# Mixer of a hybrid encoder: three engines in a written order, the softmax's sum and maximum in one instruction, the gates' first products inside attention

## The chip, the cores and the metric

The kernel runs on one core of one Trainium2 chip. The metric is the device time of one execution in microseconds. A core has five engines with a queue each: TensorE (PE, matmuls; its weight loads are shown as PEld), VectorE (DVE), ScalarE (ACT), GpSimd (POOL) and SyncE (SP, which here only issues DMAs). An engine works through its queue in order and waits at an instruction until what it needs has arrived. SBUF is the memory on the chip, and PSUM is where matmuls write, here as 8 banks.

## The reference

Two layers, each of three residual steps, and a final RMSNorm; 512 tokens of 1024 numbers, all in float32:

```python
def mixer(h, w_in, gate_bias, rpb, w_na_out, w_f_out, w_o):
    z = h @ w_in                      # q, k, v: 512 columns each, uf: 512, ga and gf: 1024 each
    ...
    y_na = neighbourhood_attention(q, k, v, rpb) @ w_na_out
    y_f = fourier_mix(uf) @ w_f_out   # real part of a 2-D DFT, 4 groups of 128 channels
    g_na = jax.nn.sigmoid(ga + gate_bias[0])
    g_f = jax.nn.sigmoid(gf + gate_bias[1])
    return (g_na * y_na + g_f * y_f) @ w_o

for l in range(DEPTH):                # DEPTH = 2
    x = x + 0.5 * swiglu(rms_norm(x, ffn1_norm[l]), ffn1_w_in[l], ffn1_w_out[l])
    x = x + mixer(rms_norm(x, mix_norm[l]), ...)
    x = x + 0.5 * swiglu(rms_norm(x, ffn2_norm[l]), ffn2_w_in[l], ffn2_w_out[l])
return rms_norm(x, final_norm)
```

SwiGLU has a hidden width of 2816. The attention has 8 heads of 64; a token of the 8 x 64 grid looks at 8 rows and 16 columns around it, and a learned bias by relative position is added to the scores before the softmax.

## The kernel before, in words

**Precision.** Each float32 operand is split into a high part, which ACT rounds to the matmul's input format, and a low part, which DVE takes as the difference (`split`, lines 297 to 300: L299 is the ACT half, L300 the DVE half). A product is three matmuls, high by high, high by low and low by high (`mm3`, L293 to L295). So every weight granule (128 x 1024, 512 KB) is loaded, rounded by ACT and subtracted by DVE before TensorE can use it, and so is every activation.

**The stream of weights.** `Stream` holds all granules in the order of their use. `next()` hands out one and prepares (`Item.prep`: the split, and a sum of two granules where one is needed, L173) two more ahead (AHEAD); `fetch` issues the loads of FETCH = 8 granules beyond what is prepared. Loads are DMAs on SP's queue (L150); sums of two granules are done either by DVE or by an accumulating DMA on POOL's queue (L152 and L182), which first waits for the plain load. Split granules lie in three rotating pairs (`wp`), or, for the four V granules (`kept=True`), in general slots, of which there are 23 of 4 KB per partition (`kp`). Most large products go by Strassen's scheme: seven products of half-size blocks instead of eight, with an order of their own (`ORDER`, products 1, 5, 2, 6, 7, 3, 4), where sums of the input blocks are products' operands and the outputs are added to and subtracted from each other.

**A layer.** FFN 1, mixer, FFN 2. FFN's output product ends with Strassen's product 4 in three chunks (`m == 4`), after which the last quarter of x (half 1 of the columns, token blocks 0 and 1) is final. The mixer's normalisation needs, for each pair of token blocks j, the sums of squares over all columns (`squares`, ACT), the inverse root by 13 small DVE steps on two columns (`roots`), x scaled by it (`scale`, ACT, L390), and then for each quarter (i, j) (half i of the columns, pair j of the blocks) the transposition by TensorE and ACT (`quad`, L375 and L378) and the split into xh and xl.

**The mixer** (`stage_mixer`) runs: V projection (`proj_V`, token blocks 2 and 3 first, then 0 and 1, then a store to `vd`, from which `vc` is gathered again in another order); sums and differences of mirrored positions (`fold`), the Fourier branch's input projection (`proj_U`, sums ue and differences uo), its transform over positions (`four_pos`) and over channels (`four_ch`, outputs pf and qf); the four pairs of heads' q and k projections (`proj_q`, `proj_k`), between them the attention in eight steps, two for each pair of heads. `att_step(i)` issues the output of step i-2 (`att_out`), the transposition of the probabilities of step i-1 (`att_trans`) and the scores of step i with their softmax (`att_scores`). The last steps alternate with the Fourier branch's output projection, eight rows of it (`f_fill`, whose w at L1103 and L1104 holds the weight rows of the middle channel). Then come the attention's output projection (`fill_n`), the two gate blocks (`gate_block`) and the product with w_o.

The softmax of a step, on two PSUM banks of 512 columns (two quarters of 256 keys each), is

```python
V.scalar_tensor_tensor(s_[e], ps[e], DH**-0.5, near_, ALU.mult, ALU.add)
V.tensor_reduce(nmx[...], s_[e]..., AX.X, ALU.max, negate=True)
S.activation(s_[e][:, c], s_[e][:, c], AF.Exp, bias=nmx[...], accum_out=sm[...])
V.reciprocal(rs[...], sm[...])
V.tensor_tensor(se, se, rs[...]..., ALU.mult)
```

**What sets the order.** A scheduler places the instructions of each engine by priority and by its model of when each is ready, so that an instruction can stand before one that the program names earlier. Only inside `tc.manual_schedule(engines=...)` do the named engines keep the program's order. Before the change such blocks hold DVE and ACT at a few places: in FFN's last part (scale and the quarters (1, 1) and (0, 1)), and after attention. The pool for the mixer's own tiles (`swap_pools(1)`) is opened in FFN's last part, and the one for FFN's raw weights after the last row of `f_fill`.

Of the kernel before, what the change touches and what calls it, by code (L numbers as in the profile page):

```python
# [32 lines left out]
FETCH = 8  # L33
# [4 lines left out]
UK = ((0, 1, 2), (3, 4, 5), (6, 7))  # L38
C_COS, C_SIN, C_ALT, C_X, C_X4, C_K = 0, 256, 512, 520, 776, 780
# [53 lines left out]
def encoder_kernel(  # L93
# [91 lines left out]
    def stage_items():  # L185
# [44 lines left out]
        for l in range(L):  # L230
# [4 lines left out]
            for g in range(4):  # L235
                add(Raw((s, "v", g)), kept=True)
# [20 lines left out]
    class Stream:  # L257
# [11 lines left out]
        def prep(self, to):  # L269
            n = len(self.items)  # L270
            while self.prepped < min(to, n) and self.items[self.prepped].stage <= self.stage:
                self.fetch(self.prepped + FETCH)
                self.items[self.prepped].prep()
                self.prepped += 1

        def enter(self, stage):
            self.stage = stage
            self.fetch(self.prepped + FETCH)
# [4 lines left out]
        def next(self):  # L283
            self.prep(self.pos + 1 + AHEAD)
# [37 lines left out]
    class Norm:  # L322
# [41 lines left out]
        def quad(self, i, j):  # L364
            self.tiles(i)
# [13 lines left out]
            split(hq, lq, raw)  # L379

        def scale(self, j):

            with tc.high_priority():
                for _ in self.roots(2 * j, 2):
                    pass
            for b in range(2):
                t = self.xn[2 * j + b] = slot(F32, "xn", (D,))
                for i in range(2):
                    c = slice(i * T, (i + 1) * T)
                    S.activation(t[:, c], x[:, 2 * j + b, c], AF.Copy, scale=self.r[:, b : b + 1])  # L390
# [38 lines left out]
    def product(ps, acts, kts, start, stop=True, again=False, hook=None, by_block=False):  # L429
# [4 lines left out]
        if by_block:  # L434
            w = [ws.next() for _ in range((len(kts) + 1) // 2)]
            for b in range(2):
                for i, kt in enumerate(kts):
# [3 lines left out]
                    mm3(ps[b], h[:, kt, c], l[:, kt, c], wh[:, z], wl[:, z], start and i == 0, last, again)  # L441
            return
# [53 lines left out]
    def stage_ffn(norm, nxt, late):  # L496
# [194 lines left out]

        ps = {}
        for i, (m, c, _) in enumerate(steps):
            make(i)
            if i:
                make(i + 1)
            key = {6: 1, 4: 7}.get(m, m)
            if key not in ps:
                ps[key] = pair(f"o{key}")
            if m == 4 and c == 0 and nxt.mix:  # L700
                make(i + 2)
                ws.finish_stage()
                swap_pools(1)
# [6 lines left out]
            if m == 4 and c == 0 and not late:  # L710
                with tc.manual_schedule(engines={mybir.EngineType.DVE, mybir.EngineType.Activation}):
                    make(i + 2)
                    if nxt.mix:
                        nxt.scale(1)
# [67 lines left out]
            else:  # L782
                update(ps[7], 1, 0, 1)
                nxt.squares(1, 0)
                if not nxt.mix:
                    nxt.later((1, 0))
# [27 lines left out]
    def stage_mixer(l, norm, nxt):  # L814
        mp = mix_pool[0]
# [23 lines left out]
        def parted(ps, s, order, **n):  # L839

            hi, lo = hilo(s)
# [723 lines left out]
```

## Time and profile before

| | |
|---|---|
| time, median of 3 runs | 1977.5 us (1970.16 to 1980.21) |
| profiled execution | 1967.59 us, of which span 1965.6 us |
| TensorE busy | 1900.5 us (97%) |
| VectorE, ScalarE, GpSimd busy | 1539.6, 1149.6 and 169.4 us |
| HBM read | 370.90 MB |
| granted TensorE clock, mean | 0.984 |

In the lines that follow, a row of the timeline gives start, duration, engine, source line, operation, output and inputs by the names of the program, and the shape; in brackets stands the idle time of the engine just before it and what ended it. A row `A <- B: total, times, longest` of the waits says that A stood still for B. A matmul's duration overlaps with the next one's, so its pace is read from start to start. The granted clock is 1.00 at full speed. L299 and L300 are lines of a helper: tiles say what is split.

### The profile page before, as it was taken

Reading aid. Unit: us, or ns where it says so; the run is one execution under the profiler, and the core shown is the slowest. Engines: PE = TensorE matmul, PEld = TensorE weight load, DVE = VectorE, ACT = ScalarE, POOL = GpSimd, SP = SyncE. Lnnn points to the kernel's source line nnn. Section 1 sums busy time; section 2 is a strip of 40 time slices with the busy share of each in tenths; the row PEclk is TensorE's granted clock in tenths of the full one; section 3 lists DMA queues with packets and bytes.
Section 4 is the critical chain, followed back from the end, with each engine's and each line's share of the span. In section 5 each row is a group of like instructions: output and inputs, shape, how many; then the busy total and the mean of one; then the engine's idle time right before and its main releaser. Section 6 shows DMA issues by size and latency. Waiting matters only on the chain.

```text
span 1965.6 us, 25798 instructions
## 1 busy us (share of the span) xinstructions
PE 1900.5 (97%) x9609; PEld 1599.7 (81%) x9609; DVE 1539.6 (78%) x1842; ACT 1149.6 (58%) x1684; POOL 169.4 (9%) x204
## 2 busy tenths in 40 slices
PE   9999999899999999999999999989889999999997
PEld 7788887778898888888888888868678988888885
DVE  7767798659768866779977778984687787677898
ACT  6655655646555755565655556564465666555654
POOL 0001011000111010101001000110001110010010
PEclk9999999899999999999999999989899999999998
DMA  8677499550987567749857656985319975776593
GB/s 280 194 201 193 149 257 290 192 154 28 253 230 198 135 186 206 186 153 265 236 144 206 182 162 182 284 287 162 101 56 261 247 178 138 202 190 172 173 280 120
DMA packets 108285, 378.88 MB, mean 193 GB/s; under 512 B 12280, under 2 KB 12408, under 8 KB 108160
## 3 DMA queue, kind: packets, MB, share of 16 engines
q1 hardware_dynamic: 80080, 279.35, 40.4%
q0 software_dynamic: 27648, 97.59, 27.1%
q8 instruction: 75, 1.23, 0.2%
q14 instruction: 50, 0.41, 0.1%
q10 hardware_dynamic: 432, 0.30, 0.1%
HBM read 370.90 MB, written 6.29 MB: 192 GB/s over the span
## 4 chain that ended last, share of the span: by engine, by line
PE 67%; DVE 15%; DMA 8%; issue 5%; ACT 4%; SPq 0%; POOL 0%; ACTq 0%; DVEq 0%; POOLq 0%
DMA raw<-in_wst_dram 7%; PE A L293 7%; PE A L294 7%; PE A L295 7%; DVE wlo L300 5%; PE B L293 4%; PE B L295 4%; PE B L294 4%; PE o L294 2%; PE o L295 2%; PE ps L293 2%; PE o L293 2%; PE ps L294 2%; PE ps L295 2%; PE C L294 2%
## 5 line engine op out<-in xcount | busy, mean ns | idle before, releaser
L300 DVE TENSOR_TENSOR wlo<-raw,whi 128x1024 fp32r<-128x1024 f32 (+1 forms) x524 | 619.9, 1189 | 307.6 <-ACT whi L299 305.2
L299 ACT ACTIVATE whi<-raw 128x1024 fp32r<-128x1024 f32 (+1 forms) x524 | 539.4, 1034 | 482.8 <-PE A L295 116.3
L152 POOL DMA_DIRECT2D raw<-in_wst_dram x162 | 140.4, 881 | 1496.2 <-DMA raw<-in_wst_dram 658.9
L173 DVE TENSOR_TENSOR raw<-raw,raw 128x1024 f32<-128x1024 f32 (+1 forms) x136 | 160.6, 1190 | 17.9 <-DMA raw<-in_wst_dram 15.4
L295 PE MATMUL A<-whi,xl 128*128 128x512 f32 x320 | 124.6, 389 | 0.0
L293 PE MATMUL A<-whi,xh 128*128 128x512 f32 x320 | 124.5, 389 | 0.0
L294 PE MATMUL A<-wlo,xh 128*128 128x512 f32 x320 | 124.5, 389 | 0.0
L175 ACT ACTIVATE whi<-raw 128x1024 fp32r<-128x1024 f32 x76 | 79.0, 1039 | 71.5 <-PE B L295 33.2
L176 DVE SCALAR_TENSOR_TENSOR wlo<-raw,whi 128x1024 fp32r<-128x1024 f32 x76 | 90.4, 1194 | 17.8 <-ACT whi L175 17.8
L489 ACT ACTIVATE sn<-A 128x512 f32<-128x512 f32 x96 | 57.0, 599 | 41.6 <-PE A L295 40.1
L295 PEld LDWEIGHTS A<-whi,xl 128*128 128x128 f32 x320 | 60.1, 188 | 12.5
L293 PEld LDWEIGHTS A<-whi,xh 128*128 128x128 f32 x320 | 60.1, 188 | 12.5
L294 PEld LDWEIGHTS A<-wlo,xh 128*128 128x128 f32 x320 | 60.1, 188 | 12.5
L293 PE MATMUL B<-whi,t1h 128*128 128x512 f32 x160 | 63.7, 398 | 0.0
L293 PE MATMUL A<-whi,t3h 128*128 128x512 f32 x160 | 62.4, 390 | 1.3 <-ACT sn L489 1.3
L294 PE MATMUL C<-wlo,xh 128*128 128x512 f32 x160 | 62.4, 390 | 0.5 <-DVE wlo L300 0.5
L294 PE MATMUL A<-wlo,t2h 128*128 128x512 f32 x160 | 62.4, 390 | 0.4 <-DVE wlo L300 0.4
L295 PE MATMUL B<-whi,t1l 128*128 128x512 f32 x160 | 62.4, 390 | 0.0
L295 PE MATMUL A<-whi,t2l 128*128 128x512 f32 x160 | 62.3, 389 | 0.0
L294 PE MATMUL A<-wlo,t3h 128*128 128x512 f32 x160 | 62.3, 389 | 0.0
L294 PE MATMUL B<-wlo,t1h 128*128 128x512 f32 x160 | 62.3, 389 | 0.0
L295 PE MATMUL C<-whi,xl 128*128 128x512 f32 x160 | 62.3, 389 | 0.0
(426 smaller groups left out, 5265.9 us busy)
## 6 DMA issues: line engine op xcount, KB each, us to landing
raw<-in_wst_dram SPq DMA_DIRECT2D x467, 512.0 KB
raw<-in_wst_dram POOLq DMA_DIRECT2D x172, 512.0 KB, 8.1
raw<-in_wst_dram SPq DMA_DIRECT2D x30, 256.0 KB
vc<-vd SPq DMA_DIRECT2D x28, 256.0 KB
bm<-in_near_dram SPq DMA_DIRECT2D x16, 384.0 KB
vd<-v SPq DMA_DIRECT2D x8, 512.0 KB
dft<-in_dft_dram POOLq DMA_DIRECT2D x4, 514.0 KB, 13.1
x<-in_xin_dram SPq DMA_DIRECT2D x4, 512.0 KB
```

Of the source, the lines that this page charges most:

```text
L152: G.dma_start(out=self.t, in_=wst[GRAN_AT[self.plus]][:, 0 : self.n], accum_op=ALU.add)
L173: V.tensor_tensor(t, t, self.add.t, self.op)
L175: S.activation(hi, t, AF.Copy, scale=-1.0)
L176: V.scalar_tensor_tensor(lo, t, -1.0, hi.bitcast(F32), ALU.mult, ALU.subtract)
L293: PE.matmul(ps, lh, rh, start=start, stop=False, skip_group_check=again)
L294: PE.matmul(ps, lh, rl, start=False, stop=False, skip_group_check=again)
L295: PE.matmul(ps, ll, rh, start=False, stop=stop, skip_group_check=again)
L299: S.activation(hi, src, AF.Copy)
L300: return V.tensor_tensor(lo, src, hi.bitcast(F32), ALU.subtract)
L489: S.activation(t[:, b, :], ps[b], AF.Copy)
```

## The change

- The three engines DVE, ACT and PE keep the program's order from FFN's last part (`last_part`, new) to attention's last step; POOL and SP remain with the scheduler. The order itself is new.
- FFN's last part: `roots` is issued behind the first granule of chunk 0, the scaling behind the first of chunk 1, quarter (1, 1) behind chunk 1; chunk 2 goes block by block, with quarter (0, 1) between the two blocks, so that the last x of block 0 is final before block 1 is computed.
- V takes its granules in the order 2, 3, 0, 1 (column half 1 first) and back in the reverse order; one granule is kept instead of four. The scaling of half 0 of blocks 0 and 1 goes to DVE. Sums come behind the first pass, differences inside the second.
- `proj_q(1)` and step 0's scores go ahead of `four_ch`; the table of exponentials is loaded behind `proj_U`. Transform results pf and qf share one tile with dft's place.
- Softmax: sum and maximum are one instruction for each quarter, the bias is multiplied by 8 on POOL, and the normalising of the second bank goes to ACT.
- The first two products (1 and 2) of gate block 0 go into attention: product 1 ahead of step 8, product 2 ahead of step 9; the block's order is 1, 2, 5, 6, 7, 3, 4, and the granules of products 1 and 2 and of fill_n are loaded in the mixer's stage.
- FETCH is 4 in the mixer's stage, 8 elsewhere. The mixer's pool is opened at its start.

```diff
+ORDER_0 = (1, 2, 5, 6, 7, 3, 4)
-FETCH = 8
+FETCH = (8, 4)
+VG = (2, 3, 0, 1)
...
-            for g in range(4):
-                add(Raw((s, "v", g)), kept=True)
+            for g in VG:
+                add(Raw((s, "v", g)), kept=g == VG[0])
...
-            st += 1
+            strassen(s, lambda q: "g" + q, 0, two, ORDER_0[0:2], True)
             for g in range(2):
                 add(Raw((s, "n", 0, g)))
-            for i in range(2):
-                strassen(s, lambda q: "g" + q, i, two, ORDER, True)
+            st += 1
+            strassen(s, lambda q: "g" + q, 0, two, ORDER_0[2:], True)
+            strassen(s, lambda q: "g" + q, 1, two, ORDER, True)
...
+        def last_part(i, to):
+
+            written.append(tc.manual_schedule(engines=WRITTEN))
+            written[-1].__enter__()
+            raw_pool[0] = mix_raw
+            ws.enter(ws.stage + 1)
+            n = [list(range(len(CHUNK[0][c]))) for c in range(3)]
+
+            def root():
+                make(i + 2)
+                for _ in nxt.roots(2, 2):
+                    pass
+
+            product(to, made.pop(i), n[0], False, False, True, hook=root)
+
+            def scaled_half():
+                for k in (1, 0):
+                    nxt.scale(1, k)
+
+            product(to, made.pop(i + 1), n[1], False, False, True, hook=scaled_half)
+            update(ps[1], 1, 0, 1)
+            nxt.quad(1, 1)
+            lower = []
+
+            def between():
+                lower.append(nxt.quad_steps(0, 1))
+                next(lower[0])
+
+            product(to, made.pop(i + 2), n[2], False, True, True, by_block=True, hook=between)
+            update(to, 1, 0, 1, (0,))
+            nxt.squares(1, 0, (0,))
+            next(lower[0])
+            update(to, 1, 0, 1, (1,))
+            nxt.squares(1, 0, (1,))
+            for _ in lower[0]:
+                pass
...
+            ws.prep(ws.pos + 3)
+            for _ in norm.roots(0, 2):
+                pass
+            norm.scale(0, 0, True)
+            norm.scale(0, 1)
             pss[2], pss[3] = bank(), bank()
...
+            for n, g in enumerate(VG):
+                w[g] = ws.next(min(AHEAD, 3 - n))
+                some((2, 3), g, n == 0, n == 3)
+                if n >= 2:
+                    low.append(norm.quad_steps(n - 2, 0))
+                    next(low[-1])
+                    next(low[-1])
+            for z in low:
+                for _ in z:
+                    pass
+            folds = [slot(F32, "ht"), slot(F32, "ht")]
+            for i in range(2):
+                a, b, t = norm.raw[i, 0], norm.raw[i, 1], folds[i]
+                V.tensor_tensor(t[:, :, 1:HALF], a[:, :, 1:HALF], b[:, :, HALF - 1 : 0 : -1], ALU.add)
+                V.tensor_copy(t[:, :, 0:1], a[:, :, 0:1])
+                hp.append(parts(t, "hp"))
             done(2)
             done(3)
...
+            for n, g in enumerate(VG[::-1]):
+                some((0, 1), g, n == 0, n == 3)
...
+                if n in (0, 1):
+                    ws.prep(ws.pos + 1 + n)
+                if n > 1:
+                    a, b = norm.raw[n - 2, 0], norm.raw[n - 2, 1]
+                    V.tensor_tensor(a[:, :, 1:HALF], a[:, :, 1:HALF], b[:, :, HALF - 1 : 0 : -1], ALU.subtract)
+                    hm.append(parts(a, "hm"))
+            ws.prep(ws.pos + 3)
             done(0)
             done(1)
...
+                G.tensor_single_scalar(res, res, DH**0.5, ALU.mult)
...
+            for e, jj, c, z in quarters:
+                V.tensor_tensor_reduce(
+                    s_[e][:, c], ps[e][:, c], bms[hp][e][:, pr + jj, :], -(DH**-0.5), 3.0e38, ALU.add, ALU.min,
+                    nmx[:, z : z + 1],
                 )
+            for e, jj, c, z in quarters:
+                S.activation(
+                    s_[e][:, c], s_[e][:, c], AF.Exp, scale=-1.0, bias=nmx[:, z : z + 1], accum_out=sm[:, z : z + 1]
+                )
+                if jj:
+                    V.reciprocal(rs[:, 2 * e : 2 * e + 2], sm[:, 2 * e : 2 * e + 2])
+            se = s_[0].rearrange("p (a k) -> p a k", a=2)
+            V.tensor_tensor(se, se, rs[:, 0:2].unsqueeze(2).to_broadcast([P, 2, 256]), ALU.mult)
+            for jj in range(2):
+                c = slice(jj * 256, (jj + 1) * 256)
+                S.activation(s_[1][:, c], s_[1][:, c], AF.Copy, scale=rs[:, 2 + jj : 3 + jj])
...
+        proj_q(1)
+        att_step(0)
         four_ch()
-        proj_q(1)
...
+        bias_for(1)
+        proj_k(1)
+        att_step(1)
+        proj_q(2)
+        bias_for(2)
+        att_step(2)
+        proj_k(2)
+        att_step(3)
+        proj_q(3)
+        bias_for(3)
+        att_step(4)
+        proj_k(3)
+        att_step(5)
         f_rows = f_fill()
+        block = gate_block(0, acts, ORDER_0, {6: lambda: fourth()}, ga0, gf0)
         for i, n in ((6, 3), (7, 3), (8, 2)):
             for _ in range(n):
                 next(f_rows)
+            if i == 8:
+                next(block)
             att_step(i)
         for _ in f_rows:
             pass
         swap_pools(0)
+        next(block)
         att_step(9)
+        written.pop().__exit__(None, None, None)
...
+    WRITTEN = {mybir.EngineType.DVE, mybir.EngineType.Activation, mybir.EngineType.PE}
```

More of the change, by code (lines that the diff above doesn't have):

```diff
@@ L1178, in with_n @@
                 both(j)
-            for m in ORDER:
+            for m in order:
                 if m == 1:
@@ L1305, in fourth @@
             split(hx[0][:, :, 256:512], lx[0][:, :, 256:512], t12)
-        m00, m01 = gate_block(0, acts, {6: fourth})[0]
-        ga1, gf1 = gate_block(1, acts, {})
+        fill_n(0, w)
+        for _ in block:
+            pass
+        m00, m01 = ga0
+        for _ in gate_block(1, acts, ORDER, {}, ga1, gf1):
+            pass
         a1 = parts(m00, "m1")
```

166 lines of the change are left out of this document (68 added, 98 removed).

## The prediction

> **What bounds the kernel now.** First the page's head and the chain of waits of TensorE alone (columns: in total, times, longest).
>
> ```profile
> span 1965.6 us, 25798 instructions
> PE 1900.5 (97%) x9609; PEld 1599.7 (81%) x9609; DVE 1539.6 (78%) x1842; ACT 1149.6 (58%) x1684; POOL 169.4 (9%) x204
> ```
> ```profile
> PE ps L293 <- ACT xh L299: 15.5, 2, 8.6
> PE ps L1058 <- DVE rs L1045: 5.3, 4, 1.4
> PE ps L981 <- ACT ce L299: 3.4, 2, 1.7
> PE ps L1058 <- ACT s L1042: 3.4, 1, 3.4
> PE tr L375 <- ACT xn L390: 2.9, 2, 1.5
> PE ps L293 <- ACT whi L299: 2.8, 2, 1.4
> PE ps L1115 <- DVE w L1104: 0.8, 2, 0.4
> ```
>
> TensorE is the bound, and the change takes no matmul away: ORDER_0 holds the seven products of ORDER. Only time in which PE waits, or runs at a lower clock, can be won. All large waits lie in the two mixers, twice each. The stretches (length, PE busy, PEld, DVE, ACT, POOL, granted clock, DMA):
>
> ```profile
> 339.00:366.00 27.00, 16.98 (x80) 13.46 (x79) 16.12 (x27) 21.24 (x38) 0.00 (x0) 0.81 0.66 201
> 366.00:396.00 30.00, 30.00 (x186) 26.55 (x185) 21.13 (x25) 14.63 (x23) 0.88 (x1) 1.00 0.59 200
> 396.00:422.00 26.00, 23.53 (x105) 18.05 (x104) 8.56 (x16) 6.85 (x15) 0.87 (x1) 0.87 0.72 216
> 422.00:466.00 44.00, 43.89 (x270) 36.66 (x268) 39.47 (x67) 28.00 (x69) 0.95 (x1) 1.00 0.17 48
> 466.00:502.00 36.00, 30.10 (x220) 26.30 (x219) 31.10 (x64) 23.16 (x63) 0.00 (x0) 0.93 0.23 83
> 1308.00:1336.00 28.00, 19.62 (x89) 15.50 (x88) 16.38 (x28) 22.49 (x40) 0.00 (x0) 0.82 0.48 180
> 1366.00:1392.00 26.00, 23.53 (x112) 17.75 (x110) 8.36 (x15) 7.61 (x17) 0.00 (x0) 0.87 0.74 206
> 1392.00:1408.00 16.00, 12.65 (x51) 9.61 (x52) 12.68 (x20) 7.12 (x17) 0.88 (x1) 0.79 0.27 55
> 1442.00:1475.00 33.00, 27.52 (x204) 24.52 (x203) 27.96 (x59) 20.25 (x60) 0.00 (x0) 0.95 0.18 66
> ```
>
> Where PE idles, the clock drops too. PE's timeline shows what that costs:
>
> ```profile
> 325.14 0.39 PE L293 MATMUL o<-whi,c4h 128*128 128x512 f32 x1
> ...
> 339.87 0.39 PE L295 MATMUL o<-whi,c4l 128*128 128x512 f32 x1
> ...
> 352.42 0.80 PE L293 MATMUL ps<-whi,xh 128*128 128x512 f32 x1 [8.55 <-ACT xh L299]
> ...
> 357.18 0.40 PE L295 MATMUL ps<-whi,xl 128*128 128x512 f32 x1
> ...
> 378.28 0.28 PE L293 MATMUL ue<-whi,hh 128*128 128x260 f32 x1
> ...
> 385.95 0.28 PE L293 MATMUL uo<-whi,hh 128*128 128x256 f32 x1
> ...
> 391.70 0.40 PE L293 MATMUL ps<-xh,whi 128*128 128x512 f32 x1
> ```
>
> The 66 matmuls of FFN's last part start every 0.227 us (14.73/65). After the long wait eleven take 4.76 instead of 2.50: 2.3 us more.
>
> **What goes (both mixers).** *FFN to V*: waits 15.5 + 2.9 and twice the 2.3: 23.0. Now quad(1,1) and quad(0,1) stand before and inside the last chunk, and V begins with the granules of half 1, so 24 matmuls (5.4 us) pass before half 0 is needed. *four_ch*: idle 2.5, and 26 x 0.13 = 3.4 at the lower clock, twice: 11.8. proj_k(0), proj_q(1) and the first scores now stand between four_pos and four_ch: 48 x 0.227 = 10.9 us of cover. *First transposes of the second mixer*: 3.35 + 16 x 0.21 = 6.7. Their cause is on DVE: a weight sum done ahead of its time, behind which the softmax was queued.
>
> ```profile
> 1390.30 1.22 DVE L173 TENSOR_TENSOR raw<-raw,raw 128x1024 f32<-128x1024 f32 x1 [7.88 <-DMA raw<-in_wst_dram]
> ```
>
> In a written order this sum comes two granules before its use. *Attention's end*: 5.9 + 36 x 0.07 and 5.5 + 33 x 0.05: 15.5. The 48 matmuls of product 1 (5.8 us at the 0.12 of the uo rows, 5.75/48) and those of product 2 now lie before the transposes and outputs that waited. Together 57.0.
>
> **What comes.** The durations:
>
> ```profile
> 334.38 0.15 DVE L319 SCALAR_TENSOR_TENSOR r<-rt,r 128x2 f32<-128x2 f32 x1
> ...
> 335.55 0.16 DVE L319 SCALAR_TENSOR_TENSOR r<-rt,r 128x2 f32<-128x2 f32 x1
> ...
> 357.25 2.36 DVE L300 TENSOR_TENSOR wlo<-raw,whi 128x1024 fp32r<-128x1024 f32 x2 [0.56 <-ACT whi L299]
> ```
> ```profile
> 340.36 2.54 ACT L390 ACTIVATE xn<-x,r 128x512 f32<-128x512 f32 x4
> ...
> 345.09 1.55 ACT L378 ACTIVATE xr<-tr,gn 128x256 f32<-128x256 f32 x4
> ...
> 356.17 2.00 ACT L299 ACTIVATE whi<-raw 128x1024 fp32r<-128x1024 f32 x2
> ```
>
> A small DVE step costs 0.195 when it depends on the last (1.17/6), the 13 of roots 2.5 us; wide steps in a row start every 1.15 us on DVE (two end after 2.36, one lasts 1.22) and every 0.95 on ACT (two end after 2.00). In the written regions DVE stands still for each ACT half of a split (about 1 us), where the scheduler had put other work in.
>
> *a) roots in the last part.* On DVE, from chunk 0's start: the update of ps[3] to 0.8, a weight's low half to 2.4, the chunk's difference, ACT's high half and the low half to 5.8, roots to 8.3, then the low half of chunk 1's second granule to 9.4. PE wants it after 31 matmuls, at 7.0: 2.4 us each time, 4.8. Low end 0 (before, roots were spread over this stretch without a wait), high end 8 with a lower clock.
>
> *b) V and U.* Let 0 be the first V matmul. DVE in order: update of x and the low half of (0,1) to 2.8, a weight to 4.4, roots to 7.0, scaling to 8.0, a weight to 10.2, quads (0,0) and (1,0) to 12.8 and 16.8 (the second waits for PE's transposes and ACT's 1.55 + 1.05), two sums with splits to 23.6, V's low halves to 24.8, two U weights to 26.6, two differences with splits to 33, the third U weight to 34, V's others to 35, the um weights to 38.4 and 41.7. PE could start V's fourth granule at 9.0, U at 24.5, its third granule at 30.3 and uo at 32.2 (from the ue and uo rows: 7.7 and 5.75). That is about 1 us at V and 6 at U. Low end 2 a mixer, since the scheduler's row 366:396 has DVE busy 21.1 of 30 without a wait; high end 10. I take 6, nearest the added durations: 12.
>
> *c) f_fill's w.* Its copies now stand behind the softmax of step 5 on ACT, and the seventh matmul of row 0 needs them.
>
> ```profile
> 468.63 1.28 DVE L1035 SCALAR_TENSOR_TENSOR s<-ps,bm 128x512 f32<-128x512 f32 x2
> 469.83 1.27 DVE L1036 TENSOR_REDUCE nmx<-s 128x2 f32<-128x512 f32 x2
> ...
> 471.13 1.22 DVE L1104 TENSOR_TENSOR w<-r,w 4x1024 fp32r<-4x1024 f32 x1
> ```
> ```profile
> 469.06 2.13 ACT L1103 ACTIVATE w<-r 4x1024 fp32r<-4x1024 f32 x2
> ...
> 471.21 0.51 ACT L1042 ACTIVATE s<-s,nmx 128x256 f32<-128x256 f32 x1
> ```
>
> From the end of the scores: the low halves of p to 0.5, the first of the four new instructions to 0.9, four exponentials to 2.9, reciprocal and two ACT copies to 3.8, w's copies to 4.9 or 5.9, DVE's 1.22 to 6.1 or 7.2. PE is there after 0.7: 5.4 to 6.5 us, I take 5.6, and 1.4 at the lower clock, twice: 14.0. Low end 0.4 a mixer (the wait of L1115 before), high end 9.
>
> *d) Gates.* Product 1's second granule is prepared behind step 7's softmax and two rows (1.0), and the output of the last head is split behind product 2's difference and four tanh (0.8): 3.6; from 0 to 8. Block 0's product 6 now follows 5 at once, but both granules of 5 are prepared before fill_n, whose 48 matmuls (10.9 us) cover the added transfer.
>
> *Softmax in one.* The two pairs take 2.55 us a step. No tensor_tensor_reduce is in the trace: four of 256 columns cost at least half the two first ops (0.64), at most the 2.55 and four accumulator reads of a small step (3.3); I take 1.7. Half of the normalising goes to ACT. Row 422:466 has PE 43.89 of 44, so neither reaches the path: 0, and were the cover gone, 0.8 a step.
> *Moved loads and queues.* Opening the mixer's pool at its start, not in FFN's last part, puts the loads of dft, fc and bm on POOL's and SP's queues behind FFN's last granules:
>
> ```profile
> dft<-in_dft_dram POOLq DMA_DIRECT2D x4, 514.0 KB, 13.1
> ```
> They land 13.1 us later; four_pos needs them after U, 39.3 us behind the first V matmul (352.42 to 391.70): 0, and what is over 39 us without that cover. FETCH 4 has seven granules on their way before use (four fetched, three prepared), each lasting 12 matmuls or 2.7 us in V and twice that in q and k: 19 us, above the 13.1: 0; without it each late granule costs PE its lateness, and DVE in order as at 1390.30. The weights of products 1 and 2 and of n (six granules) come into slots ahead of the change of pools; pf and qf in one tile, V kept once instead of four times and ex outside make room for them: 0. The table for exponentials is loaded behind U on ACT, where q's projection (5.4 us) covers it: 0.
>
> Sum: 57.0 - (4.8 + 12 + 14 + 3.6 = 34.4) = 22.6. The profiled execution took 1967.6 (span and 2.0 around it), 9.9 below the median of 1977.5, which is also the 0.5% that a measurement can tell from no change. Against the median: **1955**.
>
> [...] After 8.55 us of idling the matmuls ran at half pace. [...]
>
> **Rivals.**
> 1. *The new waits are mostly hidden.* Row 366:396 speaks for it, the in-order sums against it. With 10 us of the 34 left: 1977.5 - 47 = 1930. Chance 0.22.
> 2. *Given back in full.* a to d at their upper ends, 8 + 20 + 18 + 8 = 54, against 57: 1974. Chance 0.16.
> 3. *Slower, by POOL's queue.* The bias is now multiplied on POOL before it is used, and a POOL queue stands behind an accumulating load until that may start:
>
> ```profile
> 332.64 0.53 POOL L917 MEMSET ux<- 128x512 f32 x1 [29.79 <-DVE wlo L300]
> ...
> 391.46 0.88 POOL L152 DMA_DIRECT2D raw<-in_wst_dram  x1 [53.14 <-DMA vc<-vd]
> ```
> If two multiplications of a mixer queue behind such a wait, DVE's softmax and then PE stand. It decides from 11.3 us a mixer on; with 20 each, 1995. Against it: each bias is asked for two projections and an attention step ahead of its use, 48 matmuls of 0.227 and what lies between, at least 10.9 us. Chance 0.15.
> 4. [...] Chance 0.07.
>
> **How the numbers follow.** The forecast has 0.40, its own range 1940 to 1967. Faster: 0.40 + 0.22 + 0.07 = 0.69; same 0.16 (rival 2); slower 0.15. Range 1924 to 1984: rival 1 and some below it, rival 2 and the near part of rival 3.
>
> **What would show it.** No PE wait over 3 us on xh or xn; four_ch with no wait on ce. Waits of U's matmuls on DVE wlo of some 2 us each and one of w (L1115) of about 5 us a mixer would show b and c; their absence rival 1. DVE waiting for POOL on the bias shows rival 3. The weakest step is b, a sum of some thirty durations.

## The result and the profile after

The changed kernel takes 1985.4 us (median of 13 runs), the kernel before 1970.6 in the same series: a ratio of 1.0078, 95% interval 1.0057 to 1.0100. It is slower by 0.8%; the forecast was faster by 1.1%. The profiled execution takes 1984.4 us.

The head of its page, and TensorE's waits (columns as in the prediction: total, times, longest):

```profile
span 1982.6 us, 25852 instructions
PE 1897.3 (96%) x9609; PEld 1602.1 (81%) x9609; DVE 1524.3 (77%) x1894; ACT 1161.3 (59%) x1710; POOL 206.5 (10%) x220
```
```profile
PE ps L1173 <- DVE w L1162: 16.3, 2, 8.2
PE ps L296 <- ACT whi L302: 11.9, 3, 5.8
PE A L487 <- ACT whi L302: 8.2, 3, 3.9
PE o L297 <- DVE wlo L303: 8.1, 7, 3.2
PE A L487 <- ACT whi L177: 4.7, 2, 2.4
PE ue L296 <- ACT whi L302: 3.9, 4, 1.3
PE ue L297 <- DVE wlo L303: 3.6, 4, 1.0
```

(After the change the halves of a split are L302 and L303.) The waits that the change was to take away are gone: xh, ce, and s and rs at the transpositions. In their place, every PE wait above 1.5 us in total is for a weight, but for the one at the program's start (L140, 3.2), which the kernel before has too. The stretches that answer to those quoted before, and two behind them (length, PE, PEld, DVE, ACT, POOL, granted clock, DMA):

```profile
339.00:366.00 27.00, 24.86 (x118) 20.14 (x117) 18.65 (x30) 14.09 (x26) 10.37 (x8) 1.00 0.48 136
366.00:396.00 30.00, 24.98 (x152) 20.94 (x151) 20.76 (x24) 15.75 (x27) 0.00 (x0) 0.94 0.71 264
396.00:422.00 26.00, 26.00 (x142) 20.63 (x141) 12.05 (x28) 11.86 (x29) 0.91 (x1) 1.00 0.79 213
422.00:466.00 44.00, 37.51 (x244) 32.02 (x242) 30.21 (x83) 29.80 (x77) 10.38 (x6) 0.98 0.39 114
466.00:520.00 54.00, 43.02 (x306) 40.66 (x307) 32.59 (x66) 29.30 (x67) 3.99 (x5) 0.86 0.39 117
520.00:550.00 30.00, 26.12 (x171) 24.21 (x170) 24.73 (x23) 15.30 (x19) 3.98 (x6) 0.94 0.92 211
...
1445.00:1500.00 55.00, 40.13 (x293) 38.52 (x294) 32.09 (x71) 31.64 (x76) 2.63 (x3) 0.82 0.32 98
```

FFN to V (339:366) now has PE idle 2.1 instead of 10.0; V and U (366:396) have 5.0, where there was none, and 396:422, where four_ch waited, has none. From f_fill's first row on (the end of 422:466, and 466:520) PE idles 6.5 and 11.0, with the clock at 0.86; in the second mixer 14.9 of 55 at 0.82.

To compare kernels whose order differs, a sum over PE's timeline serves: for each matmul the time from its start to the next one's, less the 20th percentile of that time for its shape. It holds idle time and lower clock alike; "lost" below means this. It also holds some 8 us of each middle part that are neither (the changed kernel has no wait there and a clock of 1.00, and still 7.9), so only differences of it count. A mixer is cut in three: from FFN's last part to q's first matmul, from there to f_fill's first row, and from there to the product with w_o (first and second mixer, us):

```
                        to q          to f_fill      to w_o        sum
before              13.2  12.4     14.5  20.9     15.9  15.6      92.5
changed             14.3  16.7      7.9   7.8     32.1  34.4     113.2
```

The 20.7 us between the sums stand against 17.0 between the spans. The middle part wins 19.7, the last loses 35.0, and the first, in which most was to be won, 5.4 more than before. Where the last part is lost is seen on the timelines of the first mixer. ACT, then DVE, then PE, about w:

```profile
464.37 0.91 ACT L1107 ACTIVATE s<-s,rs 128x256 f32<-128x256 f32 x2 [0.23 <-DVE rs L1102]
465.18 2.12 ACT L1161 ACTIVATE w<-r 4x1024 fp32r<-4x1024 f32 x2
...
483.93 1.06 ACT L302 ACTIVATE whi<-raw 128x1024 fp32r<-128x1024 f32 x1 [0.96 <-DVE raw L175]
```
```profile
460.40 1.29 DVE L303 TENSOR_TENSOR p<-ps,p 128x512 fp32r<-128x512 f32 x2 [0.19 <-ACT p L302]
461.60 0.41 DVE L1093 CUSTOM_DVE_ANT_0 s<-ps,bm 128x256 f32<-128x256 f32 x1
461.94 0.08 DVE L1093 DVE_READ_ACCUMULATOR2_ANT nmx<- 128x1 f32 x1
461.94 0.42 DVE L1093 CUSTOM_DVE_ANT_0 s<-ps,bm 128x256 f32<-128x256 f32 x1
...
466.25 1.22 DVE L1162 TENSOR_TENSOR w<-r,w 4x1024 fp32r<-4x1024 f32 x1 [1.33 <-ACT w L1161]
...
482.68 1.21 DVE L175 TENSOR_TENSOR raw<-raw,raw 128x1024 f32<-128x1024 f32 x1
```
```profile
458.52 0.39 PE L296 MATMUL ps<-pq,whi 128*128 128x258 f32 x1
...
467.61 0.55 PE L1173 MATMUL ps<-p,w 68*128 68x258 f32 x1 [8.10 <-DVE w L1162]
...
485.04 0.58 PE L296 MATMUL ps<-pq,whi 128*128 128x256 f32 x1 [5.77 <-ACT whi L302]
...
502.80 0.39 PE L487 MATMUL A<-xh,whi 128*128 128x256 f32 x1 [2.38 <-ACT whi L177]
```

w's copies stand behind the normalising of step 5's softmax, as forecast. The wait at 485.04 is a second one of the same kind: the last difference granule of f_fill (sum L175, ACT at 483.93) stands behind step 6's softmax and the copies of a row's output, since the change asks one granule less ahead there (`ws.next(AHEAD - 1)`). The third is product 1's second granule, behind step 7's softmax. Later product 6 of block 0 waits for its weight, and that for a transfer (POOL's issue, then ACT):

```profile
519.49 0.86 POOL L184 DMA_DIRECT2D raw<-in_wst_dram  x1 [2.40 <-DVE wlo L303]
```
```profile
533.79 1.06 ACT L302 ACTIVATE whi<-raw 128x1024 fp32r<-128x1024 f32 x1 [3.57 <-DMA raw<-in_wst_dram]
```

### The profile page after: what moved, and what is told of

The parts are those of the page before. It is cut to its first block, busy times and chain, and to the rows that moved or that the text cites. A ratio compares the mean times of both kernels' runs of the same rounds, so it can differ in the third digit from the quotient of the medians.

```text
span 1982.6 us, 25852 instructions
## 1 busy us (share of the span) xinstructions
PE 1897.3 (96%) x9609; PEld 1602.1 (81%) x9609; DVE 1524.3 (77%) x1894; ACT 1161.3 (59%) x1710; POOL 206.5 (10%) x220
## 3 DMA queue, kind: packets, MB, share of 16 engines
q8 instruction: 75, 1.23, 0.3%
## 4 chain that ended last, share of the span: by engine, by line
PE 67%; DVE 17%; ACT 6%; DMA 5%; issue 5%; SPq 0%; POOL 0%; DVEq 0%; ACTq 0%; POOLq 0%
PE A L296 7%; PE A L298 7%; PE A L297 7%; DVE wlo L303 5%; DMA raw<-in_wst_dram 5%; PE B L298 4%; PE B L296 4%; PE B L297 4%; PE o L297 2%; PE o L298 2%; PE o L296 2%; PE ps L296 2%; PE ps L298 2%; PE ps L297 2%; PE C L297 2%
## 5 line engine op out<-in xcount | busy, mean ns | idle before, releaser
L303 DVE TENSOR_TENSOR wlo<-raw,whi 128x1024 fp32r<-128x1024 f32 (+2 forms) x524 | 621.0, 1192 | 299.5 <-ACT whi L302 297.8
L302 ACT ACTIVATE whi<-raw 128x1024 fp32r<-128x1024 f32 (+2 forms) x524 | 539.2, 1034 | 447.3 <-PE A L298 116.0
L175 DVE TENSOR_TENSOR raw<-raw,raw 128x1024 f32<-128x1024 f32 (+1 forms) x136 | 160.6, 1190 | 2.5
L296 PEld LDWEIGHTS A<-whi,xh 128*128 128x128 f32 x320 | 60.1, 188 | 12.4
L297 PE MATMUL C<-wlo,xh 128*128 128x512 f32 x160 | 62.4, 390 | 0.5 <-DVE wlo L303 0.5
L297 PE MATMUL A<-wlo,t2h 128*128 128x512 f32 x160 | 62.4, 390 | 0.4 <-DVE wlo L303 0.4
L296 PE MATMUL A<-whi,t3h 128*128 128x512 f32 x160 | 62.4, 390 | 0.2 <-ACT sn L505 0.2
L296 PE MATMUL C<-whi,xh 128*128 128x512 f32 x160 | 62.2, 390 | 0.2 <-ACT whi L302 0.2
L298 PE MATMUL B<-whi,t1l 128*128 128x512 f32 x160 | 62.4, 390 | 0.0
```

What stands on the lines that cost most here:

```text
L175: V.tensor_tensor(t, t, self.add.t, self.op)
L296: PE.matmul(ps, lh, rh, start=start, stop=False, skip_group_check=again)
L297: PE.matmul(ps, lh, rl, start=False, stop=False, skip_group_check=again)
L298: PE.matmul(ps, ll, rh, start=False, stop=stop, skip_group_check=again)
L302: S.activation(hi, src, AF.Copy)
L303: return V.tensor_tensor(lo, src, hi.bitcast(F32), ALU.subtract)
```

## The experiments

Three theories. Theory 1: weights are late by their place in the order written out, and each wait is worth its length. Theory 2: loads are late, since the mixer's stage asks for four ahead and the next stage's loads are all asked for at its start. Theory 3: the softmax in one instruction costs the time, on POOL and ACT. Ratios are to the kernel before, measured again beside each group of runs, with 95% intervals. Its median went from 1970.0 to 1973.0 between groups, so a difference of less than 3 us between two runs of different groups says little.

**One wait at a time.** w's rows are prepared behind step 4:

```diff
         att_step(4)
+        w64 = w_rows()          # cut out of f_fill
         proj_k(3)
```

> The changed kernel, with the preparation of f_fill's w (memset, load, two ACT copies, one DVE step) moved from behind the scores of step 5 to behind those of step 4, so that ACT has it ahead of step 5's softmax. Theory 1 (the written order put new waits in PE's way, each worth its own length): the wait of the w matmul, 8.2 us in each mixer, goes, and with it some 2 us at the lower clock: 18 us less than the changed kernel's 1985, about 1967 (1964 to 1973). Theory 2 (weights arrive late in this stretch, whatever the order, since fewer are requested ahead): PE only gets to the next late weight sooner, and no more than 6 us are won. Theory 3 (the softmax in one instruction with its bias on POOL and its copies on ACT is what costs): nothing of the loss is here, but the wait itself would still shrink by the 2 us that w's copies take.

1983.9 us, 1.0063 (1.0039 to 1.0087). w's wait is gone from the list and next to nothing is won. Its waits of PE:

```profile
PE ps L296 <- ACT whi L302: 14.9, 4, 7.1
```

f_fill's last difference granule waits 7.1 instead of 5.8, and small waits for weights and copies, and slower matmuls, take the rest: the last part of the mixers loses 31.3 and 33.3 instead of 32.1 and 34.4. Of the 16.3 some 9 come back as other idle time of that part (PE's idle times there sum to 36.7, instead of 43.8) and 5 as slower matmuls. So this wait, taken away, is not worth its length.

The other one: f_fill's rows are dealt four, four and none to steps 6, 7 and 8, and the granule is prepared ahead of step 6's softmax:

```diff
-        for i, n in ((6, 3), (7, 3), (8, 2)):
+        for i, n in ((6, 4), (7, 4), (8, 0)):
             for _ in range(n):
                 next(f_rows)
+            if i == 6:
+                ws.prep(ws.pos + 2)
```

> The changed kernel, with the rows of f_fill dealt 4, 4 and 0 to the three last steps, not 3, 3 and 2, and the second weight of the second half prepared right behind the fourth row, ahead of step 6's softmax. Theory 1: the wait on ACT whi of 5.9 us in each mixer (row 4, behind step 6's softmax on DVE and ACT) goes: 12 us less than 1985, about 1973 (1970 to 1979). Theory 2: that weight is late by its load, the wait stays or moves to the next weight: at most 3 us won. Theory 3: no change beyond 3 us.

1983.4 us, 1.0058 (1.0036 to 1.0081). The same picture: the granule's wait of 5.8 is gone, product 1's second granule waits 5.2 in place of 2.4.

```profile
PE A L487 <- ACT whi L177: 10.3, 2, 5.2
```

Roots and U: the next weights are prepared ahead of the roots in FFN's last part, and in the mixer V's low halves and the mirrored differences go behind the preparation of U's weights:

```diff
             def root():
                 make(i + 2)
+                ws.prep(ws.pos + 3)
...
-            done(2)
-            done(3)                      # V's splits, now behind U's weights
...
-                if n > 1:
-                    ... differences, split      # now behind done(0), done(1)
```

> The changed kernel with two orders on DVE and ACT altered: in FFN's last part the next two weights are prepared ahead of roots, and in V the two sums come before their splits, V's own splits and the differences behind the U weights. Theory 1: the waits on wlo in FFN's last part (2.7 and 3.3 us) go, and of the waits inside U (about 6 us a mixer) half, since DVE's sum of work there stays the same: 6 + 6 = 12 us less than 1985, about 1973 (1969 to 1980). Theory 2: U's weights are late by their loads and only the 6 us of roots are won. Theory 3: as theory 2, or nothing.

1977.3 us, 1.0034 (1.0012 to 1.0056): 8 less than the changed kernel. In the profiled execution the first part loses 12.8 and 9.8 (from 14.3 and 16.7): 8.4 won, as much as the medians differ by. The last part loses 38.9 and 34.7 there (from 32.1 and 34.4), but this execution, at 1981.9, is 4.6 above the median, and the waits in that part are the same within 1.5 us; nearly all of the 7.1 are slower matmuls. So it isn't shown that a later weight takes the gain back.

All three edits together:

> The three edits together. Theory 1: 18 + 12 + 12 = 42 us less than 1985, about 1943 (1937 to 1955), below the kernel before (1971) by 1.4%. Theory 2: the parts don't add up, since late loads take the place of the waits: not below 1965. Theory 3: not below 1960.

1972.2 us, 0.9995 (0.9977 to 1.0013): 13 less than the changed kernel, about the sum of what the three gave one by one (1.5, 2 and 8), and far from the sum of their waits. The last part still loses 30.6 and 31.1. What is late now:

```profile
PE A L487 <- ACT whi L177: 11.5, 2, 5.7
PE A L487 <- ACT whi L302: 7.2, 2, 3.6
```

With product 1's second granule prepared ahead of step 7's softmax as well:

```diff
+            if i == 7:
+                ws.prep(ws.pos + 2)
             att_step(i)
```

> The changed kernel with the three earlier edits together (w early, second frequency granules early, roots behind weights), and product 1's second granule prepared before step 7's softmax as well. Theory 1: the wait of product 1 (11.5 in all) goes, and with it some clock: 1958 to 1963 (from 1972). Theory 2: product 6, whose loads come no earlier, waits longer by as much (7.2 to some 15): 1968 to 1972.

1961.4 us, 0.9945 (0.9923 to 0.9967): 11 less, for a wait of 11.5, as theory 1 has it; product 6, the next in the chain, waits little longer (8.4 in place of 7.2). That the two numbers agree is in part luck. Of the 8.9 that the last part loses less between the two profiled executions, idle time makes 3.6, as smaller waits took the place of the rest, and fewer slow matmuls make 5.3. And product 6 without the accumulating load behind product 5 (its granules are loaded and added to afresh):

```diff
+            d6 = [Raw((s, name("d"), idx, g), n, (s, name("a"), idx, g)) ...]
...
+                    if own and m == 5:
+                        add(d)
+                    elif own and m in (3, 6):
+                        add(d6[g], then=b.key if m == 6 else None)
```

> The kernel of the run before in this list, and product 6 of block 0 no longer waits for an accumulating load behind product 5's preparation: its two granules are loaded whole and added to from the start of the stage. Theory 1: product 6's wait (7.2 in all, or what has come to it) goes: 1950 to 1960. Theory 2: there are two more granules in the same burst of loads, so a weight of n, 5 or 6 is late by DMA all the same: no better than the run before, 1958 to 1972, with a wait of whi on DMA over 3 us in it.

1961.1 us, 0.9948 (0.9927 to 0.9970). This kernel leaves a summand, c, out of the weights of block 0's products 6 and 3; a full one would need one accumulating load more. Product 6 waits no more, and the median is the same. A part of the wait has moved on to product 3 (B on xh):

```profile
PE B L492 <- ACT whi L307: 3.4, 2, 2.6
```
```profile
1510.27 2.00 ACT L307 ACTIVATE whi<-raw 128x1024 fp32r<-128x1024 f32 x2 [6.18 <-DMA raw<-in_wst_dram]
```

ACT waits 6.18 for a transfer behind product 6, in a stretch whose DMA share was 0.92 in the changed kernel (520:550). So product 6's own wait was for its accumulating load. That the loads of the stage's start (theory 2) limit what follows is likely, but not shown: no run asks for them earlier. In any case, all that product 6 loses in the changed kernel is 9.4 of the last part's 66.5.

**Parts undone.** Gates' products back behind attention, in the old order:

```diff
-            strassen(s, lambda q: "g" + q, 0, two, ORDER_0[0:2], True)
+            st += 1
             for g in range(2):
                 add(Raw((s, "n", 0, g)))
-            st += 1
-            strassen(s, lambda q: "g" + q, 0, two, ORDER_0[2:], True)
+            strassen(s, lambda q: "g" + q, 0, two, ORDER, True)
...
-            if i == 8:
-                next(block)
...
```

> The changed kernel, with the gates' products 1 and 2 put back behind attention and the order 1, 5, 2, 6 again. Theory 1 (a weight late by its place in the written order): the waits of product 1's second granule (4.7 in all) and of product 6 (8.2) go, and the idle time at attention's end, which the products covered, comes back (before: 15.5 with its clock): 1984 to 1990. Theory 2 (the loads of the next stage, all asked for at once, are late): product 6 is 48 matmuls further off, its wait goes too, but the loads of 5 or of n are late instead: a wait of whi on DMA over 3 us stays, 1985 to 1995. Theory 3 (softmax in one costs the time): nothing of it is changed, 1985.

1981.6 us, 1.0060 (1.0034 to 1.0087), a little below what was expected. The waits of products 1 and 6 are gone, those of w and of f_fill's granule stand as they were, and what comes back at attention's end is 7.0:

```profile
PE ps L1172 <- DVE w L1161: 16.5, 2, 8.2
...
PE ps L295 <- ACT p L301: 7.0, 2, 3.5
```

The last part loses 1.2 less in all. So the gates' move is worth about nothing, where the prediction had 15.5 - 3.6.

The softmax of the change alone, in the kernel before:

```diff
-                V.scalar_tensor_tensor(s_[e], ps[e], DH**-0.5, near_, ALU.mult, ALU.add)
-                V.tensor_reduce(nmx[...], ..., ALU.max, negate=True)
+                V.tensor_tensor_reduce(s_[e][:, c], ps[e][:, c], bms[hp][e][...], -(DH**-0.5), 3.0e38, ALU.add, ALU.min, nmx[...])
...
+                G.tensor_single_scalar(res, res, DH**0.5, ALU.mult)
...
```

> The kernel before, with only the softmax of the change: sum and maximum in one instruction, the bias multiplied on POOL, half of the normalising on ACT. Theories 1 and 2: hidden work of DVE alone, 1966 to 1972 (from 1971), with a gain at most where a weight waited behind a softmax on DVE. Theory 3 (the new softmax costs time, by POOL's 2.1 us a bias and ACT's two added copies): over 1976.

1968.0 us, 0.9966 (0.9930 to 1.0003). Theory 3 falls: in that kernel it costs nothing and may win up to 0.7%.

**The order itself.** No order written out from FFN's last part to attention's end; every other line as changed:

```diff
-            written.append(tc.manual_schedule(engines=WRITTEN))
-            written[-1].__enter__()
...
-        written.pop().__exit__(None, None, None)
```

> The changed kernel without the order written out on the three engines: the same instructions, which the scheduler sets in its own order (the three inner places that were written out before stay). Theory 1 (the order written out puts preparations of weights behind long chains): the waits of w (16.3), of the second frequency granule (11.9 with others) and of product 1 go, and the chains that the written order had taken away (x's roots and transposes, before 18.4; four_ch 5.9) may come back in part: 1965 to 1980. Theory 2 (loads late after the change of pools): product 6's wait of 8 stays whatever the order, 1975 to 1985. Theory 3 (softmax): by the run of the kernel before with the new softmax it fell; nothing here.

1940.4 us, 0.9835 (0.9798 to 0.9873): 45 us below the changed kernel, and far below what either theory gave. Ended at f_fill's first row instead:

```diff
         f_rows = f_fill()
+        written.pop().__exit__(None, None, None)
...
-        written.pop().__exit__(None, None, None)
```

> The changed kernel with the written order ended at f_fill, ahead of its first row, instead of after the last attention step. Theory 1: the waits that the changed kernel has from there on (w 16.3, second frequency granule about 12, product 1 4.7) are the scheduler's to avoid, while the gains up to there (7 to 9 us a mixer at the first row) stay: 1955 to 1970. Theory 2: product 6 stays late, and takes what is won: 1975 to 1985.

1950.9 us, 0.9895 (0.9862 to 0.9928). Its list of PE's waits:

```profile
PE o L297 <- DVE wlo L303: 8.5, 7, 3.1
PE A L487 <- ACT whi L302: 6.5, 4, 3.2
...
PE ps L1173 <- ACT w L1161: 2.1, 2, 1.0
```

w's wait falls from 16.3 to 2.1, and the granule's from 5.8 each to at most 0.4; the last part loses 14.1 and 15.9. What the scheduler does is seen on its ACT:

```profile
464.41 0.49 ACT L1098 ACTIVATE s<-s,nmx 128x256 f32<-128x256 f32 x1
...
464.90 1.04 ACT L1161 ACTIVATE w<-r 4x1024 fp32r<-4x1024 f32 x1
465.85 0.89 ACT L1107 ACTIVATE s<-s,rs 128x256 f32<-128x256 f32 x2
466.75 1.05 ACT L1161 ACTIVATE w<-r 4x1024 fp32r<-4x1024 f32 x1
...
471.50 1.06 ACT L302 ACTIVATE whi<-raw 128x1024 fp32r<-128x1024 f32 x1
472.47 1.05 ACT L177 ACTIVATE whi<-raw 128x1024 fp32r<-128x1024 f32 x1
473.42 0.49 ACT L1098 ACTIVATE s<-s,nmx 128x256 f32<-128x256 f32 x1
```

w is no earlier than in the changed kernel (its second copy ends at 467.80, there at 467.30). But PE takes 36 matmuls of the rows that need no w, then a head's 12 outputs and four transpositions (9.25 us from the first row's start) before the first matmul with w. And two granules are prepared ahead of step 6's exponentials, in ACT's time that the written order leaves idle.

Ended there, and with w's rows and the edits of roots and U:

> The run before in this list, and w's rows prepared behind step 4, roots behind the next weights, and V's low halves and differences behind U's weights. Theory 1: another 7 to 10 below the run before in this list, as roots and U's edits gave 8 in the changed kernel alone: 1945 to 1962. Theory 2: no better than 1961, since the loads set when the products can start.

1939.0 us, 0.9839 (0.9808 to 0.9869). Here the edits give 12 by the medians, 7 between the profiled executions. The first part loses 9.1 less, and the last what it did (14.5 and 16.1).

Which engine's order is it? Written out on PE alone, then on DVE and ACT alone:

```diff
-    WRITTEN = {mybir.EngineType.DVE, mybir.EngineType.Activation, mybir.EngineType.PE}
+    WRITTEN = {mybir.EngineType.PE}
```

> The changed kernel with the order written out on PE alone; DVE and ACT are set by the scheduler. In the run that ended the written order at f_fill, PE took 36 matmuls of the rows and a head's 12 outputs ahead of the first that needs w, and w's two copies stood between the softmax's instructions. Theory 1a (the order of PE is what makes the late weights cost): w's wait stays, near 16 in all, 1975 to 1985. Theory 1b (the order of DVE and ACT is what makes weights late): the waits of w and of the second frequency granule shrink to under 3 each: 1942 to 1955.

> The changed kernel with the order written out on DVE and ACT alone; PE is set by the scheduler. Theory 1a: PE takes other rows and outputs while w and the second frequency granule are prepared, 1942 to 1955. Theory 1b: the weights are as late as in the changed kernel, and PE has little else by then: 1970 to 1985.

PE alone: 1967.1 us, 0.9979 (0.9950 to 1.0008). DVE and ACT alone: 1973.3 us, 1.0005 (0.9983 to 1.0027). PE's waits in the first and in the second:

```profile
PE ps L1173 <- ACT w L1161: 12.4, 2, 6.2
PE A L487 <- ACT whi L302: 8.9, 4, 3.9
PE ps L1116 <- ACT s L1098: 8.0, 2, 6.4
```
```profile
PE ps L296 <- ACT whi L302: 14.5, 3, 7.3
PE A L487 <- ACT whi L302: 9.9, 4, 4.4
...
PE ps L1173 <- DVE w L1162: 3.8, 2, 1.9
```

Both theories are half right, and the two waits part: w is a matter of PE's order (it stays at 12.4 with PE's written out, falls to 3.8 with PE free), f_fill's granule one of DVE's and ACT's (it stays at 14.5 with theirs written out, and is not among the large ones with theirs free). Of the 45 us between the changed kernel and the free one, freeing two engines gives 18, freeing PE 12; the other 15 come only when all three are free.

Last, no order written out, and the edits of w's rows, roots and U:

> The changed kernel without the order written out at all, and with the edits of roots, V and U, and w's rows behind step 4. Theory 1: as w's and U's waits are short already where the scheduler sets the order, nothing is left to win: 1936 to 1943. Were their work itself, not its order, on the path: under 1932.

1924.2 us, 0.9771 (0.9721 to 0.9821), the best of all: 2.3% under the kernel before. The forecast of "nothing left to win" was wrong. The time lies in the range given for work on the path (under 1932), but the edits take no work away, so that reading is not shown either. The sums of what is lost:

```
                        to q          to f_fill      to w_o        sum
all three edits     11.7   9.8      7.8   7.8     30.6  31.1      98.8
ended at f_fill     14.4  15.7      7.9   7.9     14.1  15.9      75.9
PE alone             9.5  11.6     18.0  12.4     21.3  23.3      96.1
DVE, ACT alone      13.3  15.2      8.0   9.5     28.0  29.9     103.9
not written out      6.5   7.7     12.5  20.8     12.3  13.3      73.1
same, and edits      3.7   4.5      9.7   9.0     12.5  12.3      51.7
```

From the changed kernel to the last the sum falls by 61.5, the span by 62.4 (1982.6 to 1920.2). Against the kernel without edits 5.9 comes in the first part, which the edits touch, and 14.7 in the middle, where that kernel has one wait of 9.9 on a softmax:

```profile
PE ps L1114 <- ACT s L1096: 11.8, 2, 9.9
```

How much of the latter the edits do, and how much is the scheduler's luck with another program order, no run tells.

## Why the prediction was wrong

**What goes, 57.0.** The waits are gone as said. By the table the middle part wins 19.7, against 11.8 + 6.7 for four_ch and the first transpositions. *Attention's end* (15.5) went too, but the products moved there wait 16.5 themselves (*d* below), so that undoing the move changes little.

**What comes, 34.4.** Measured as time lost in the changed kernel, both mixers together:
- *a) roots in the last part*: 2.7 and 3.3, and 1.2 of lower clock (0.50 in 1314.42:1316.94): 7.2 against 4.8. Right, slightly small.
- *b) V and U*, called the weakest step: at V 2.8 and 2.1, at U 6.7 and 6.9, in all 18.5 against 12. The mechanism and the places were right, U's 6 too; V's 1 was small, and its upper end of 10 a mixer held.
- *c) f_fill's w*: 8.3 and 8.4, and 3.5 of lower clock (0.50 in 467.60:471.30): 20.1 against 14. The chain and PE's arrival ("after 0.7": the row starts at 458.52, the wait ends at 467.61 after 8.10, so after 1.0) were right; its first link was not. "The low halves of p to 0.5" end 3.1 after the scores (461.60), since the copies of o and p, which alternate between ACT and DVE, stand ahead of the softmax; the rest takes 5.9 (461.60 to 467.47), as in the sum (6.1 or 7.2, less 0.5).
- *Missed: f_fill's last difference granule*, 5.9 in each mixer and 7.1 in the slow matmuls behind it (clock 0.50 in 485.00:491.80): 19.0, priced at nothing. Its cause is a line of the change that the diff above leaves out, `(eh, el), (oh, ol) = ws.next(), ws.next(AHEAD - 1)` in f_fill, and no cost was given to it. It is the largest error of any term.
- *d) gates*: product 1's second granule costs 3.6 a mixer, 7.1 against 2; the split of the last head costs nothing. Product 6, priced at 0 since fill_n's "48 matmuls (10.9 us) cover the added transfer", loses 4.0 and 5.4: its accumulating load took from 519.49 to about 533.8, 14 us, among the loads that the change of pools sets off (DMA share 0.98 in 519.49:533.80). The cover was named rightly; the length of what it was to hide was not worked out.

Together 81.3 against 34.4, or 46.9 too little; the profiled executions differ by +16.8 where -22.6 was forecast, or by 39.4. Of the 7.5 between these, 3.6 are gains that were forecast too small (by the same sums the three parts win 20.3, 19.7 and 20.6 beside these losses, 60.6 against 57.0), and 3.9 lie outside the three parts.

**Costed at nothing, rightly.** *Softmax in one*: four instructions take 1.4 us a step, where 1.7 was estimated, and the run in the kernel before shows no cost. *Moved loads*: no wait of PE for dft or the bias is in the list. *FETCH 4*: no weight of the mixer's stage waits for a transfer.

**Rivals.** 1 (mostly hidden, 1930) did not happen; that the same instructions take 1940 when no order is written out is another matter. 2 (given back in full) comes nearest: the items that a to d named come to 52.9, against its 54, and the 28.4 beyond them are the two costs put at nothing. 3 named the right side for a wrong reason: POOL waits 13.34 for the bias's load and multiplies for 2.12 us, but DVE waits for it nowhere. 4, given 0.07, was the author's estimate that DVE's splits are held while POOL multiplies; no row of the kernel before shows that. In the changed kernel eight splits of a weight on DVE run beside such a multiplication, and five of them take 1.32 to 1.85 us, where the 554 others of that size take 1.21 to 1.23. No wait of PE can be put down to it, and the new softmax in the kernel before costs nothing.

```profile
446.49 2.12 POOL L1070 TENSOR_SCALAR bm<-bm 128x768 f32<-128x768 f32 x1 [13.34 <-DMA bm<-in_near_dram]
```

**The step that failed** is "What comes", 34.4, which measured 81.3. Two of its costs were put at nothing: f_fill's last difference granule, for which no term stands (19.0), and block 0's product 6, whose accumulating load was taken as covered (9.4). Without these two the change would have come out 4 us faster (57.0 less 52.9) to 12 (28.4 less 16.8), as an estimate from these sums; with them it is slower. The other terms had the place right and the size too small: w by 6, V and U by 6.5, product 1 by 5.

Adding the waits up was not the error: the measured terms, added, do give a slower kernel. What a sum doesn't give is the worth of a fix. Taking away waits of 16.3 and 11.8 in the last part won 1.5 and 2, because other waits and slower matmuls took their place; ending the written order where the late weights begin won 34.

**The order of queues.** PE stands 8.10 us at one matmul with w (467.61), and the row's next matmuls, which need no w, start behind it. In the run that ends the written order at f_fill, the 36 matmuls of the rows and a head's 12 outputs, none of which needs w, stand ahead of it, and w's waits are 2.1 in all instead of 16.3.

**The clock.** Behind the waits of 8.1 and 5.8 in the first mixer, matmuls of 256 columns start every 0.21 us instead of 0.12, for 3.7 and 6.8 us (granted clock 0.50 in both stretches), and behind that of 3.2 at the second mixer's roots six start every 0.43 us instead of 0.23, while behind those of 2.4 at product 1 and 2.5 at the first mixer's roots there is no such stretch (clock 1.00 in 502.80:507.00 and 332.06:335.00). But the clock is low behind shorter waits too. In U of the first mixer the longest is 1.29, after 0.64 and 0.85 and ahead of 0.96 (at 378.95), and behind them the clock is 0.50:

```profile
377.61 0.39 PE L296 MATMUL ue<-whi,hph 128*128 128x260 f32 x1 [1.29 <-ACT whi L302]
```
```profile
379.20:382.60 3.40, 3.35 (x16) 2.56 (x15) 2.22 (x4) 1.06 (x1) 0.00 (x0) 0.50 0.75 295
```

Row 396:422 of the kernel before shows the same: PE idle 2.5, its longest wait 1.68 (on ce, at 409.35), and a clock of 0.87. How long or how many the waits must be, no run here tells.

## What to carry to other kernels

An order written out on several engines turns every preparation into a link of one chain: go through the engines' program order from each softmax or reduction to the next weight, and list for each weight what stands ahead of it, above all where the number asked for ahead is lowered. What such waits cost can be added up, but a fix of one can be worth less than its length, since the next late weight and slower matmuls take part of it (here 1.5 and 2 us were won of waits of 16.3 and 11.8); the test that tells most is to give the order back, to one engine at a time. The same program with its order left to the scheduler (1940, and 1924 with the edits of w's rows, roots and U) was far faster here than with its order written out (1985).

## What was not expected of the hardware

- A tensor_tensor_reduce of 128 x 256 is two instructions on DVE, 0.41 and 0.08 us, and starts anew every 0.34 us: the four of a step take 1.4 us, where sum and maximum took 2.55 before.
- GpSimd takes 2.12 us for one multiplication of 128 x 768 numbers by a constant, where 0.8 was the estimate from a memset of 128 x 512 (0.53 x 1.5).
- An accumulating load of 512 KB that takes 7.6 us in the median took 14 where all loads of a stage are asked for at once (issued at 519.49; DMA share 0.98 in 519.49:533.80).

```profile
raw<-in_wst_dram POOLq DMA_DIRECT2D x172, 512.0 KB, 7.6
```
